# First steps of attention: another order for the first projections, the keys' transposes and the rotations, the first modulation unit ahead of them, and the weight ring to match

## The chip, the cores and the metric

The kernel runs on one core of a Trainium2 chip. The metric is the device time of one launch in microseconds (us). The core's engines are PE (TensorE, matrix products and transposes), DVE (VectorE), ACT (ScalarE), POOL (GpSimd) and SP (SyncE, which issues the transfers). Each engine works through its own list in order, and waits there for what an instruction needs from another engine or from a transfer.

## The reference, cut to what matters

One trunk layer for 128 context tokens and 512 latent tokens of width 1024:

```
u = rms_norm(h) * g_pre1 * (1 + scale1) + shift1
q, k, v, b, c, x, g_att, g_conv = split(u @ w_in)
q, k = rms_norm per head (q_norm, k_norm); axial rotary on latent tokens only
A  = softmax(q k^T / 8) v @ w_att_out     16 query heads, 4 key heads, head width 64
Bm = (b * dwconv3(c * x)) @ w_conv_out
h  = h + gate1 * rms_norm((sigmoid(g_att) * A + sigmoid(g_conv) * Bm) @ w_o)
h  = h + gate2 * rms_norm((silu(g) * val) @ w_down),   [g, val] = dwconv3(u2 @ w_up)
```

Latent tokens attend to all latent keys and 128 cached keys; context tokens read context tokens alone. The six modulation vectors (scale, shift and gate for both halves) come from `silu(c) @ w_ada + b_ada`, once for `c` and once for `c_ctx`. Outputs are both token groups and the context keys and values.

## The kernel before, in words

All tokens are five tiles of 128: tile 0 is context, tiles 1 to 4 are latent. Products are made in three passes on rounded operands (`mm3`, lines 159 to 162: high by high, low by high, high by low), so a weight unit is cut into a high part (a copy on ACT, `whi`) and a low part (a subtraction on DVE, `wlo`), out of a raw tile of 512 KB; there are three raw tiles and three of each part.

The prologue normalises the tokens, makes the first modulation and the keys and values of all tiles (`kv_mm`). Then comes the attention stage, whose lists on PE, ACT and DVE are written out by hand: they run in the order in which the code records them. Its parts:

- Per tile of keys: `k_rotate` (DVE, for some tiles the last sum on POOL) applies the rotary tables to the product in PSUM, `k_copies` (ACT) squares it and copies the values, `k_factors` (a reduction on DVE, then a scaling and a power on POOL, lines 460 to 462) gives the norm factor, `k_double` (line 561) writes the scaled keys twice side by side, on POOL for tiles 1 and 2 (line 564), on ACT for the others (line 567). `k_into` transposes them on PE (line 371), then `k_done` makes the high part on ACT (line 377: KCH, KH) and the low part on DVE (line 378: KCL, KL).
- Per tile of queries of one head group: `q_part` is the projection on PE (24 products of 256 columns for eight blocks of the width; lines 160 to 162), `q_rotate` the rotary on DVE with its sum on POOL (lines 447 to 450), `squares` on ACT (line 454) and `factors` as for keys, `q_turn` the transposes on PE (line 485) with high part on ACT (488) and low part on DVE (491). The first three query tiles of group 0 go through `q_first`, `q_rotate_first` and `q_factors`.
- A `Step` makes the scores of 128 queries for two heads on PE (line 499), then `most` (maxima, DVE, lines 636 and 638), `exps` (ACT, line 651), `shares` (reciprocal on DVE, line 660, product on POOL, line 661), `turned` (five transposes on PE, line 674, and a copy, line 679) and, after both halves of the queries, `values` (line 698). Step 0 of a group is its context step (lines 631, 645, 656, 657, 669). The code calls a step (g, i): group g from 0 to 3, i from 0 to 8. A step transposes the probabilities of the step before it. Between these, steps carry the projections of later query tiles, `cut_hi` of a weight unit (lines 599 and 602, at the places listed in `CUTS`) and one modulation unit (`ada_use`).
- A modulation unit is two raw tiles of `w_ada` multiplied by the conditioning vectors on PE (`ada_mm`, line 212) and kept on DVE (copied on first use, line 231, afterwards added, line 233). 16 such units are spread over the attention stage.

Raw tiles are filled by SP in the order of the list `ring`: entries ("u", n) are weight units, ("a", n) are modulation tiles. Three loads are issued when the stage starts; each later one is recorded when a raw tile has been used (`ring_used`): two after a modulation unit, one after a low part. An entry waits on SP for the raw tile that it overwrites, and all later entries wait behind it. PSUM holds three double banks (`ps2`: scores, transposes of keys and probabilities) and two single banks (`ps1`: projections, transposes of queries, values, modulation).

The order around the change: `q_first(0)`, the keys' rotations, `k_double(0)`, `q_first(1)`, `k_into(0)`, `q_first(2)`, `k_into(2)`, `q_turn(0, 0)`, `k_into(4)`, then the projection of query tile 3 in two halves with the context step's scores and `k_into(1)` between, `k_into(3)`, `q_turn(0, 1)`, and step (0, 1). There `q_turn(0, 2)` stands right behind the scores. The first modulation unit stands at the end of step (0, 2).

Of the kernel before, what the change touches and what calls it, by code (L numbers as in the profile page):

```python
# [18 lines left out]
KT = 8  # L19
# [5 lines left out]
NKV = 4  # L25
# [39 lines left out]
def trunk_layer(ctx, tc, x_prompt, x_sample, cache_k, cache_v, c, c_ctx, w_ada, b_ada, g_pre1, g_post1, g_pre2,  # L65
# [93 lines left out]
    def mm3(out, ah, al, bh, bl, start, stop):  # L159
        PE.matmul(out, ah, bh, start=start, stop=False)  # L160
        PE.matmul(out, ah, bl, start=False, stop=False)  # L161
        PE.matmul(out, al, bh, start=False, stop=stop)  # L162
# [271 lines left out]
    with tc.tile_pool(name="att", bufs=2) as at:  # L434
# [37 lines left out]
        def q_part(pz, g, t, ks):  # L472
            sl = slice(t * 128, (t + 1) * 128)
            for k in ks:
                mm3(pz, UH[:, k, sl], UL[:, k, sl], *state["cut"][KT + 2 * g + k // 4].at(k % 4), k == 0, k == KT - 1)
# [6 lines left out]
        def q_turn(g, t, p=None):  # L482
            p = ps1() if p is None else p
            for i in range(2):
                PE.transpose(p[:, i * 128:(i + 1) * 128], qfs[g, t][:, 2 * i:2 * i + 2].rearrange("p h d -> p (h d)"), ident)
            src = p[:, 0:256].rearrange("p (i c) -> p i c", i=2)
            qh, ql = (x[g][:, :, t * 128:(t + 1) * 128] for x in (QH, QL))
            S.activation(qh, src, AF.Copy)

            def low():  # L490
                V.tensor_tensor(out=ql, in0=src, in1=qh.bitcast(F32), op=ALU.subtract)
            return low
# [15 lines left out]
        def ada_raws(a, b):  # L508
            return [("a", i) for i in range(2 * a, 2 * b)]

        ring = [("u", 10), ("u", 11)] + ada_raws(0, 4) + [("u", 12)] + ada_raws(4, 5) + [("u", 13)] + ada_raws(5, 8) + [("u", 14)]
        ring += ada_raws(8, 9) + [("u", 15)] + ada_raws(9, 13) + [("u", 16)] + ada_raws(13, 15) + [("u", 17)] + ada_raws(15, 16) + [("u", 18)]
        at_ring = [0, 0]

        def ring_load(upto):
# [13 lines left out]
        def ada_use(i):  # L529
            p = ada2_mm(i)  # L530
            ring_used(2)
            return lambda: ada2_keep(i, p, acc)
# [26 lines left out]
            factors(sqs.pop(t), rks[t])  # L559

        def k_double(t):
            if t in (1, 2):
                for i in range(2):
                    G.tensor_tensor(out=kds[t][:, :, i, :], in0=kfs[t], in1=rks[t].unsqueeze(2).broadcast_to((128, NKV, HD)), op=ALU.mult)
                return
            for h in range(NKV):
                S.activation(kds[t][:, h], kfs[t][:, h:h + 1, :].broadcast_to((128, 2, HD)), AF.Copy, scale=rks[t][:, h:h + 1])
            if t == 0:
                nc.sync.dma_start(new_v.rearrange("t h d -> t (h d)"), VV[:, 5, :])
                nc.sync.dma_start(new_k, kds[t][:, :, 0, :])  # L570

        def k_into(t):
            p = ps2()[:, 0:512]
            k_turn(t, kds[t], p)
            k_done(t, p)

        def q_first(t):
            pzs[t] = ps1()[:, 0:256]
            q_part(pzs[t], 0, t, range(KT))

        def q_rotate_first(t):
            q_rotate(pzs[t], 0, t)
            sqs["q", t] = squares(pzs[t])

        def q_factors(t):
            factors(sqs.pop(("q", t)), rq[0][:, t, :])
# [136 lines left out]
        k_copies(1)  # L723
        q_first(1)
        k_rotate(3)
        k_double(2)
        k_factors(1)
        k_copies(3)
        k_factors(3)
        q_factors(0)  # L730
        k_into(0)
        k_double(4)
        k_double(1)
        q_first(2)
        k_into(2)
        low = q_turn(0, 0, ps2())
        low()
        k_into(4)
        k_double(3)
        q_rotate_first(1)  # L740
        q_factors(1)


        pz = ps1()[:, 0:256]
        q_part(pz, 0, 3, range(4))
        last = Step(0)
        last.most(0)
        k_into(1)
        q_part(pz, 0, 3, range(4, KT))
        k_into(3)  # L750
        low = q_turn(0, 1, ps2())
        low()
        last.exps(0)
        last.shares(0)
        q_rotate_first(2)
        q_factors(2)
        q_rotate(pz, 0, 3)
        sq = squares(pz)
        after1, after2 = [], [lambda: factors(sq, rq[0][:, 3, :])]
        n_ada, halves = 0, []  # L760
        q_begin(1)
        CUTS = {(0, 1): 10, (0, 2): 11, (0, 8): 12, (1, 2): 13, (1, 8): 14, (2, 2): 15, (3, 2): 16, (3, 6): 17}
        for g in range(NKV):
            if g and g + 1 < NKV:
                q_begin(g + 1)
            for i in range(0 if g else 1, 9):
                low1, low2, late_hi, end = [], [], [], []
                st = Step(g) if i == 0 else Step(g, ((i - 1) // 4, (i - 1) // 2 % 2, (i - 1) % 2))

                first = {0: (g, 2), 1: None if g else (0, 2), 5: (g, 4)}.get(i)  # L770
                then = {2: (g, 3), 5: (g + 1, 0), 7: (g + 1, 1)}.get(i)
                if then and then[0] == NKV:
                    then = None
                if first:
                    low1.append(q_turn(*first))
                if i == 2:
                    hi, lo = values(g)
                    hi()
                    low1.append(lo)
                for h in range(1 if st.ctx else 2):  # L780
                    st.most(h)
                    st.exps(h)
                for f in low1 + halves:
                    f()
                halves = []

                qt = None
                if g + 1 < NKV and i in (3, 5, 7):
                    qt = (g + 1, (i - 3) // 2)
                elif i == 0 or i == (2 if g else 1):  # L790
                    qt = (g, 3 if i == 0 else 4)
                blk = (i - 3) // 2 if g + 1 == NKV and i in (3, 5, 7) else None
                if i in (4, 6, 8) or (i == 1 and g):
                    hi, lo = values(*((g - 1, 3) if i == 1 else (g, (i - 4) // 2)))
                    late_hi.append(hi)
                    low2.append(lo)
                if qt:
                    pz = ps1()[:, 0:256]
                    q_part(pz, *qt, range(4))
                if blk is not None:  # L800
                    c0, c1 = 256 * blk, min(256 * blk + 256, NTOK)
                    pz = ps1()[:, 0:c1 - c0]
                    gate_part(pz, c0, c1, range(4))
                st.shares(0)
                for f in after1:
                    f()
                copy = last.turned(0)
                if last.ctx:
                    copy()
                else:  # L810
                    copy(i == 2 or (qt is None and blk is None))
                for f in late_hi:
                    f()

                if qt:
                    q_part(pz, *qt, range(4, KT))
                if blk is not None:
                    gate_part(pz, c0, c1, range(4, KT))
                if not st.ctx:
                    st.shares(1)  # L820
                if (g, i) in CUTS:
                    low = cut_hi(CUTS[g, i])
                    if i == 2 and 0 < g < NKV - 1:
                        low2.append(lambda low=low: low(0, 512))
                        halves = [lambda low=low: low(512, 1024)]
                    elif i <= 2:
                        halves = [low]
                    else:
                        end.append(low)
                if then:  # L830
                    low2.insert(0, q_turn(*then))
                for f in low2:
                    f()
                for f in after2:
                    f()
                if not last.ctx:
                    last.turned(1)()
                after1, after2 = [], []
                if i in (4, 6, 8) or i == (1 if g else 2):
                    ada_use(n_ada)()  # L840
                    n_ada += 1
                for f in end:
                    f()
                if qt:
                    def rotation(pz=pz, qt=qt):
                        q_rotate(pz, *qt)
                        sq = squares(pz)
                        after2.append(lambda: factors(sq, rq[qt[0]][:, qt[1], :]))
                    if i == 2:
                        after1.append(rotation)  # L850
                    else:
                        rotation()
                if blk is not None:
                    S.activation(gate0[:, c0:c1], pz, AF.Copy)
                last = st
# [997 lines left out]
```

## Time and profile before

| what | value |
| --- | --- |
| median of 3 runs | 1165.7 us (1160.63 to 1167.91) |
| profiled execution | 1164.31 us |
| its span, first to last instruction | 1162.5 us |
| PE busy | 1127.4 us, 97% of the span |
| DVE, ACT, POOL busy | 792.5, 569.0, 152.8 us |
| TensorE clock granted, mean | 0.987 |
| moved by DMA | 129.58 MB |

The page names the engine, the source line, and the tile written and read; a busy time is a sum over instructions and says nothing yet of what sets the end. Idle time on PE with its releaser in brackets ("[3.01 <-ACT sq L454]") tells for how long PE stood and which instruction let it go on. The granted clock is 1.00 at full speed and 0.50 at half speed.

### The profile page before, as it was taken

How to read it: one execution, taken by the hardware profiler on the slowest of the kernel's cores; microseconds unless marked ns; L12 is line 12 of the kernel's file. 1: busy time of each engine (PE TensorE's matmuls, PEld its weight loads, DVE VectorE, ACT ScalarE, POOL GpSimd, SP SyncE). 2: the span in 40 equal slices, each digit the busy share in tenths (PEclk: the TensorE clock that was granted, in tenths of full speed). 3: DMA queues.
4: the chain of work that ended last, by engine and by line, in shares of the span. 5: the costliest groups of instructions: out<-in, count | busy, mean ns of one | idle time of the engine just before them, and what ended most of it. 6: DMA issues, size and time to landing. Idle time of an engine off the chain costs nothing. (4 is left out here: it accounts for less than half of the span.)

```text
span 1162.5 us, 19634 instructions
## 1 busy us (share of the span) xinstructions
PE 1127.4 (97%) x7949; PEld 1032.6 (89%) x7949; DVE 792.5 (68%) x1270; ACT 569.0 (49%) x978; POOL 152.8 (13%) x199
## 2 busy tenths in 40 slices
PE   7986999999999999999999999999999999999997
PEld 5775888887899999999999988999999999998785
DVE  4465666655554788988745447888877788778634
ACT  4254666665433544554542246555454555545432
POOL 1044565654100000000000012000000000000001
PEclk8988999999999999999999999999999999999999
DMA  9912243333322323323232543333332333315732
GB/s 274 261 46 66 85 125 108 92 110 93 99 73 63 95 74 91 92 73 97 86 109 73 199 144 123 98 114 114 102 101 90 95 114 103 113 60 165 245 102 90
DMA packets 181400, 129.58 MB, mean 111 GB/s; under 512 B 6274, under 2 KB 163518, under 8 KB 181310
## 3 DMA queue, kind: packets, MB, share of 16 engines
q1 hardware_dynamic: 181198, 128.30, 36.0%
q8 instruction: 62, 1.02, 0.4%
q14 instruction: 28, 0.23, 0.1%
q10 hardware_dynamic: 112, 0.04, 0.0%
HBM read 116.87 MB, written 11.45 MB: 110 GB/s over the span
## 5 line engine op out<-in xcount | busy, mean ns | idle before, releaser
L919 PE MATMUL b<-ZB,whi 128*128 128x322 f32 x1024 | 229.5, 311 | 1.7 <-DVE C L930 1.7
L919 PEld LDWEIGHTS b<-ZB,whi 128*128 128x128 f32 x1024 | 173.5, 189 | 5.5 <-DVE C L930 3.8
L919 PE MATMUL b<-ZB,wlo 128*128 128x322 f32 x512 | 159.4, 311 | 0.0
L919 PE MATMUL b<-MT,whi 128*128 128x320 f32 x608 | 134.2, 308 | 0.0
L919 PEld LDWEIGHTS b<-MT,whi 128*128 128x128 f32 x608 | 101.5, 188 | 0.0
L919 PEld LDWEIGHTS b<-ZB,wlo 128*128 128x128 f32 x512 | 96.2, 188 | 0.0
L919 PE MATMUL b<-MT,wlo 128*128 128x320 f32 x304 | 93.8, 308 | 0.0
L661 POOL TENSOR_TENSOR pr<-pr,sm 128x640 f32<-128x640 f32 x64 | 79.7, 1255 | 75.2 <-DVE sm L660 75.1
L906 ACT ACTIVATE whi<-SUM 128x1024 fp32r<-128x1024 f32 x40 | 42.2, 1055 | 81.6 <-DVE SUM L1373 79.2
L1403 DVE SCALAR_TENSOR_TENSOR Y<-C,cffn,Y 128x642 f32<-128x642 f32 x88 | 77.6, 884 | 1.8 <-ACT Y L1398 0.2
L135 DVE TENSOR_TENSOR wlo<-raw,whi 128x1024 fp32r<-128x1024 f32 (+1 forms) x33 | 36.1, 1094 | 60.8 <-ACT whi L134 60.4
L651 ACT ACTIVATE pr<-s,mx,rq 128x640 f32<-128x640 f32 x64 | 56.7, 885 | 40.2 <-DVE mx L638 39.6
L160 PE MATMUL s<-whi,UH 128*128 128x256 f32 (+1 forms) x200 | 67.2, 336 | 6.0 <-ACT sq L454 3.5
L919 PE MATMUL b<-UH,whi 128*128 128x320 f32 x228 | 70.5, 309 | 0.0
L919 PE MATMUL b<-UL,whi 128*128 128x320 f32 x228 | 70.4, 309 | 0.0
L919 PE MATMUL b<-UH,wlo 128*128 128x320 f32 x228 | 70.2, 308 | 0.0
L636 DVE TENSOR_REDUCE mx<-s 128x1 f32<-128x640 f32 x64 | 52.5, 821 | 23.1 <-PE s L499 22.7
L910 DVE TENSOR_TENSOR wlo<-raw,whi 128x1024 fp32r<-128x1024 f32 (+1 forms) x51 | 50.4, 1019 | 25.2 <-ACT whi L906 24.4
L906 ACT ACTIVATE whi<-WB 128x1024 fp32r<-128x1024 f32 x38 | 40.1, 1056 | 54.8 <-DVE WB L1014 54.8
L927 ACT ACTIVATE p<-b 128x322 f32<-128x322 f32 (+1 forms) x78 | 34.3, 439 | 62.1 <-PE b L919 62.1
L161 PE MATMUL s<-wlo,UH 128*128 128x256 f32 (+1 forms) x200 | 63.2, 316 | 0.4 <-DVE wlo L602 0.4
L162 PE MATMUL s<-whi,UL 128*128 128x256 f32 (+1 forms) x200 | 60.8, 316 | 0.0
(309 smaller groups left out, 2942.6 us busy)
## 6 DMA issues: line engine op xcount, KB each, us to landing
raw<-in_w_in_dram SPq DMA_DIRECT2D x48, 512.0 KB, 3.7
RAW<-in_w_up_dram SPq DMA_DIRECT2D x40, 512.0 KB, 3.9
raw<-in_w_ada_dram SPq DMA_DIRECT2D x32, 512.0 KB, 4.0
raw<-in_w_down_dram SPq DMA_DIRECT2D x22, 512.0 KB, 4.3
araw<-in_w_ada_dram SPq DMA_DIRECT2D x16, 512.0 KB, 6.7
actd<-Y SPq DMA_DIRECT2D x18, 321.0 KB, 2.4
AFB<-actd SPq DMA_DIRECT2D x18, 321.0 KB, 5.4
raw<-in_w_conv_out_dram SPq DMA_DIRECT2D x9, 512.0 KB, 4.0
```

The costliest lines, as they stand in the source:

```text
L135: V.tensor_tensor(out=lo[:, :n], in0=raw, in1=hi[:, :n].bitcast(F32), op=ALU.subtract)
L160: PE.matmul(out, ah, bh, start=start, stop=False)
L161: PE.matmul(out, ah, bl, start=False, stop=False)
L162: PE.matmul(out, al, bh, start=False, stop=stop)
L636: V.tensor_reduce(out=mx, in_=self.sc[h], axis=AX.X, op=ALU.max, negate=True)
L651: S.activation(pr, self.sc[h], AF.Exp, bias=mx, scale=rs, accum_out=sm)
L661: G.tensor_tensor(out=pr, in0=pr, in1=sm.broadcast_to((128, NTOK)), op=ALU.mult)
L906: S.activation(to[0], raw, AF.Copy)
L910: V.tensor_tensor(out=lo, in0=raw, in1=hi.bitcast(F32), op=ALU.subtract)
L919: PE.matmul(out, p[:, ws], q[:, k, :], start=start and k == 0 and n == 0, stop=stop and k == 3 and n == 2, skip_group_check=True)
L927: S.activation(t, pair[j][b], AF.Copy)
L1403: V.scalar_tensor_tensor(out=y, in0=crows(j)[i][:, d:d + NACT], scalar=cffn[:, 44 * d + o:44 * d + o + 1], in1=y, op0=ALU.mult, op1=ALU.add)
```

## The change

- `k_double(2)` runs on ACT as four scaled copies and no longer on POOL; it is recorded after `k_factors(3)` and `q_factors(0)`.
- The first modulation unit (`ada_use(0)`) is recorded right behind it, ahead of `k_into(0)`, and no longer at the end of step (0, 2). `q_rotate_first(1)` follows `k_into(0)`; `q_factors(1)` follows `q_first(2)`.
- The second half of the projection of query tile 3 goes behind `k_into(3)` and `q_turn(0, 1)`; `q_rotate_first(2)` goes ahead of `shares`.
- In step (0, 1) the projection of query tile 4 is made in one piece, and `q_turn(0, 2)` follows it.
- The ring begins with the two tiles of the first modulation unit. Unit 16 comes two modulation tiles earlier, and is cut in step (2, 8) instead of (3, 2).
- Cuts in a step with i = 2 always have their low part made in two halves, one in the step and one in the next; the cut in (0, 1) has its low part at the end of the step instead of in the next one.

```diff
-        ring = [("u", 10), ("u", 11)] + ada_raws(0, 4) + [("u", 12)] + ada_raws(4, 5) + [("u", 13)] + ada_raws(5, 8) + [("u", 14)]
-        ring += ada_raws(8, 9) + [("u", 15)] + ada_raws(9, 13) + [("u", 16)] + ada_raws(13, 15) + [("u", 17)] + ada_raws(15, 16) + [("u", 18)]
+        ring = ada_raws(0, 1) + [("u", 10), ("u", 11)] + ada_raws(1, 4) + [("u", 12)] + ada_raws(4, 5) + [("u", 13)] + ada_raws(5, 8)
+        ring += [("u", 14)] + ada_raws(8, 9) + [("u", 15)] + ada_raws(9, 12) + [("u", 16)] + ada_raws(12, 15) + [("u", 17)]
+        ring += ada_raws(15, 16) + [("u", 18)]
...
         def k_double(t):
-            if t in (1, 2):
+            if t == 1:
...
         k_rotate(3)
-        k_double(2)
         k_factors(1)
         k_copies(3)
         k_factors(3)
         q_factors(0)
+        k_double(2)
+        ada_use(0)()
         k_into(0)
+        q_rotate_first(1)
         k_double(4)
         k_double(1)
         q_first(2)
+        q_factors(1)
         k_into(2)
         low = q_turn(0, 0, ps2())
         low()
         k_into(4)
         k_double(3)
-        q_rotate_first(1)
-        q_factors(1)
-
         pz = ps1()[:, 0:256]
         q_part(pz, 0, 3, range(4))
         last = Step(0)
         last.most(0)
         k_into(1)
-        q_part(pz, 0, 3, range(4, KT))
         k_into(3)
         low = q_turn(0, 1, ps2())
         low()
+        q_part(pz, 0, 3, range(4, KT))
         last.exps(0)
+        q_rotate_first(2)
         last.shares(0)
-        q_rotate_first(2)
         q_factors(2)
...
-        n_ada, halves = 0, []
+        n_ada, halves = 1, []
-        CUTS = {(0, 1): 10, (0, 2): 11, (0, 8): 12, (1, 2): 13, (1, 8): 14, (2, 2): 15, (3, 2): 16, (3, 6): 17}
+        CUTS = {(0, 1): 10, (0, 2): 11, (0, 8): 12, (1, 2): 13, (1, 8): 14, (2, 2): 15, (2, 8): 16, (3, 6): 17}
...
-                first = {0: (g, 2), 1: None if g else (0, 2), 5: (g, 4)}.get(i)
+                first = {0: (g, 2), 5: (g, 4)}.get(i)
...
+                start = g == 0 and i == 1
                 if qt:
                     pz = ps1()[:, 0:256]
-                    q_part(pz, *qt, range(4))
+                    q_part(pz, *qt, range(KT if start else 4))
+                if start:
+                    low2.append(q_turn(0, 2))
...
-                if qt:
+                if qt and not start:
                     q_part(pz, *qt, range(4, KT))
...
-                    if i == 2 and 0 < g < NKV - 1:
+                    if i == 2:
                         low2.append(lambda low=low: low(0, 512))
                         halves = [lambda low=low: low(512, 1024)]
-                    elif i <= 2:
-                        halves = [low]
                     else:
                         end.append(low)
...
-                if i in (4, 6, 8) or i == (1 if g else 2):
+                if i in (4, 6, 8) or (i == 1 and g):
                     ada_use(n_ada)()
                     n_ada += 1
```

## The prediction

> **What bounds the kernel now.** I read the page's slices first.
>
> ```profile
> span 1162.5 us, 19634 instructions
> ...
> PE   7986999999999999999999999999999999999997
> ...
> PEclk8988999999999999999999999999999999999999
> ```
>
> PE is busy nearly throughout. A slice is 29.1 us; the fourth (87 to 116 us) shows 6 for PE and 8 for its clock: the first steps of attention, where the change lies. So I asked PE's waits for two stretches, 60 to 116 us and 114 to 300 us (the rest of attention).
>
> ```profile
> PE s L212 <- DMA raw<-in_w_ada_dram: 4.0, 1, 4.0
> PE s L160 <- ACT sq L454: 3.5, 2, 3.0
> PE s L485 <- POOL qf L450: 1.9, 1, 1.9
> PE s L499 <- DVE KL L378: 1.3, 1, 1.3
> PE s L674 <- issue: 0.7, 1, 0.7
> PE s L161 <- DVE wlo L602: 0.4, 1, 0.4
> ```
> ```profile
> PE s L162 <- DVE wlo L602: 2.7, 1, 2.7
> ```
>
> In the first steps PE stands for 11.8 us, in the other 186 us for 2.7 us. Behind that, PE sets the pace, so time won or lost in the first steps passes on in full. Idle time has a second price, which the clock shows over stretches of 3.41 us:
>
> ```profile
> 81.00:84.41 3.41, 3.41 (x22) 3.07 (x22) 0.31 (x1) 0.00 (x0) 1.50 (x3) 0.50 0.02 5
> 84.41:87.83 3.42, 3.42 (x18) 3.42 (x17) 1.24 (x3) 0.60 (x1) 0.00 (x0) 0.50 0.00 0
> 87.83:91.24 3.41, 2.03 (x18) 1.47 (x16) 1.30 (x5) 2.63 (x10) 0.02 (x1) 1.00 0.00 0
> 91.24:94.65 3.41, 1.18 (x8) 0.94 (x9) 2.86 (x10) 1.23 (x4) 3.24 (x5) 1.00 0.00 0
> 94.65:98.07 3.42, 3.42 (x18) 3.42 (x18) 1.56 (x6) 2.62 (x6) 2.61 (x3) 0.50 0.00 0
> 101.48:104.89 3.41, 1.43 (x23) 0.90 (x21) 3.38 (x9) 3.39 (x7) 1.13 (x1) 1.00 0.02 7
> 104.89:108.31 3.42, 0.63 (x12) 0.60 (x16) 0.33 (x2) 0.14 (x1) 2.55 (x4) 0.50 1.00 292
> ```
>
> The columns after the length are PE, PEld, DVE, ACT and POOL busy, then the granted clock. The clock changes at the edges of these stretches only. Where PE was busy for 1.18 of 3.41 us (35%) or 1.43 (42%), the next stretch has half clock; after 2.03 (59%) it does not. The Trainium skill (TensorE: Matmul & The Clock Gate, Part 1) has the same free-running window of 3413 ns.
>
> **The change part by part.** Times are on the clock of the trace. Up to the first row here PE's list is the same in both kernels; the other rows are step (0, 1)'s and step (0, 4)'s scores, and one whole modulation unit.
>
> ```profile
> 71.84 0.64 PE L371 MATMUL s<-ident,room 128*128 128x128 f32 x4
> ...
> 80.26 0.39 PE L160 MATMUL s<-whi,UH 128*128 128x256 f32 x1 [3.01 <-ACT sq L454]
> ...
> 89.76 0.65 PE L499 MATMUL s<-KH,QH 64*128 64x320 f32 x2 [1.29 <-DVE KL L378]
> ...
> 115.89 0.42 PE L499 MATMUL s<-KH,QH 64*128 64x320 f32 x2
> ...
> 120.52 1.08 PE L212 MATMUL s<-raw,s 128*32 128x128 f32 x32
> ```
> ```profile
> 53.57 8.76 SPq L142 DMA_DIRECT2D raw<-in_w_in_dram  x2
> ...
> 103.69 0.37 SPq L206 DMA_DIRECT2D raw<-in_w_ada_dram  x1
> ```
> ```profile
> DMA to landing us min/median/max: 3.6/4.8/7.3
> ```
> ```profile
> 71.89 1.02 POOL L462 TENSOR_TENSOR rk<-ssq,mhalf 128x4 f32<-128x4 f32 x1
> ```
> ```profile
> 73.19 1.07 DVE L460 TENSOR_REDUCE ssq<-sq 128x4 f32<-128x256 f32 x3
> ```
> ```profile
> 73.45 0.60 ACT L377 ACTIVATE KCH<-s 128x512 fp32r<-128x512 f32 x1
> 75.59 1.28 ACT L567 ACTIVATE room<-room,rk 128x128 f32<-128x128 f32 x4 [1.54 <-POOL rk L462]
> ```
>
> *Modulation unit in front, ring.* The ring's first two loads leave SP by 62.3 us; now they carry the modulation tiles. Landing even 7.3 us later (last row: all modulation loads), they are there before 71.84, so the unit costs its 1.0 us of PE and no wait. In the old place its second tile could be issued only at 103.69, when unit 10 was cut: that is the wait of 4.0 us, and it goes. What queues now on SP behind the unit is unit 11's load (issued about 72.8, cut at 97: 24 us) and the next two modulation tiles (the last issued about 93.3, behind unit 10's low part; needed in step (0, 4), after 104). Both are hidden. The copy of the unit on DVE waits for PE (72.9) with KCL and the rotary queued behind it, but DVE is there only at 74.2.
>
> *q_first(2).* It took the PSUM bank of query tile 0; now it takes the bank of the modulation unit, freed by the copy at line 231 (0.29 us), which stands on DVE behind the three reductions that end at 74.26. PE: unit to 72.9, `k_into(0)` to 73.5, then 1.0 us idle, `q_first(2)` 74.5 to 77.5. The 3.0 us wait for the squares goes, since the squares are long done when the next projection asks for that bank.
>
> *k_double(2) on ACT.* Two POOL products of 0.6 us leave POOL, so later norm factors come 1.2 us earlier there; four ACT copies (1.28 us, as in the row) start when the factor is done (72.91) and ACT free (73.5). Queued behind them on ACT is KCH, now 74.7 to 75.3 instead of 73.45; behind it on DVE KCL, then the rotary of query tile 1 (76.0 to 76.7), behind that its squares, `k_double(4)` (to 78.3) and the high part of tile 2's keys. PE asks for `k_double(4)` only at 78.35, so this is covered by `q_first(2)`; without that cover it would cost 1.2 us.
>
> The rest goes by these durations (groups of 60 to 130 us):
>
> ```profile
> L651 ACT ACTIVATE pr<-s,mx,rq 128x640 f32<-128x640 f32 x11 | 9.7, 885 | 9.7 <-DVE mx L638 9.5
> ...
> L599 ACT ACTIVATE whi<-raw 128x1024 fp32r<-128x1024 f32 x2 | 2.1, 1049 | 0.0
> ```
> ```profile
> L636 DVE TENSOR_REDUCE mx<-s 128x1 f32<-128x640 f32 x12 | 9.8, 820 | 3.8 <-PE s L499 3.8
> ...
> L378 DVE TENSOR_TENSOR KL<-s,KH 128x512 fp32r<-128x512 f32 x5 | 3.4, 688 | 5.7 <-ACT KH L377 5.7
> ...
> L602 DVE TENSOR_TENSOR wlo<-raw,whi 128x1024 fp32r<-128x1024 f32 x2 | 2.4, 1218 | 0.0
> ```
>
> *Keys and step (0, 1).* Three transposes end at 78.95, half a projection at 80.5, the context scores at 81.25, `k_into(1)` and `k_into(3)` at 82.35. `q_turn(0, 1)` waits for the bank that tile 1's low part frees: high part 0.60 (as KCH) and low part 0.69, in turn behind each transpose, 83.25: 0.9 us idle. Turn and second half of tile 3's projection end at 85.2; they cover the key's and query's low parts (83.8, 84.5), so step (0, 1)'s scores start at 85.2, without the 1.3 us wait, against 89.76. The whole projection of query tile 4 (86.2 to 89.15) then covers the POOL sum that `q_turn(0, 2)` waited 1.9 us for.
>
> *Steps (0, 2) and (0, 3).* Here something else is late. `q_turn(0, 2)`'s high part stands on ACT behind both exponentials (to 90.2): step (0, 2)'s scores start at 90.6, 0.6 us idle. Unit 10's parts (ACT to 92.0, DVE to 93.3) now stand ahead of query tile 4's rotary, whose squares (94.45) free the bank for `q_turn(0, 3)`: 1.6 us idle. The next transposes wait for the first exponential of that step (96.0, 1.2 us idle), step (0, 3)'s scores for the second and a copy on DVE (97.15, 0.45 us). In step (0, 3) the second half of unit 11's low part stands behind both maxima (102.2): 1.0 us. Then step (0, 4)'s scores start at 103.5, against 115.89: 12.4 us.
>
> A second count: old idle 11.8 us, plus work at half clock from 81.0 to 87.8, 94.65 to 98.07 and 107.7 (the end of the transfer's wait) to 111.7 (the next edge), 14.3 us of which at most half is lost, 7.15; less the new idle, 6.75 us. That gives 12.2. I take 12.
>
> *Clock.* The stretches 91.24 to 94.65 and 94.65 to 98.07 would have PE 53% and 52% busy in the new order, between the 42% that brought half clock and the 59% that didn't. Bounds are none and three stretches; one costs up to 3.41 / 2 = 1.7 us, three 5.1. I take one, being just nearer the 59%.
>
> *Unit 16 from (3, 2) to (2, 8).* Maxima mark the steps; (1, 3) and (3, 3) hold the same PE work but for the wait:
>
> ```profile
> 161.35 0.82 DVE L636 TENSOR_REDUCE mx<-s 128x1 f32<-128x640 f32 x1 [0.18 <-PE s L499]
> ...
> 166.80 0.82 DVE L636 TENSOR_REDUCE mx<-s 128x1 f32<-128x640 f32 x1 [0.91 <-PE s L499]
> ```
> ```profile
> 260.94 0.82 DVE L636 TENSOR_REDUCE mx<-s 128x1 f32<-128x640 f32 x1 [0.78 <-PE s L499]
> ...
> 270.73 0.82 DVE L636 TENSOR_REDUCE mx<-s 128x1 f32<-128x640 f32 x1 [5.05 <-PE s L499]
> ```
> ```profile
> 132.96 0.52 SPq L142 DMA_DIRECT2D raw<-in_w_in_dram  x1
> ```
> ```profile
> 142.83 1.06 ACT L599 ACTIVATE whi<-raw 128x1024 fp32r<-128x1024 f32 x1
> ```
>
> 9.79 against 5.45 us: the wait of 2.7 us for the low part behind the maxima, and the half clock after it, cost 4.3 us, and both go. The cut in (2, 8) is what (0, 8) does now: load issued at 132.96, high part at 142.83, 9.9 us of cover, and no PE wait there. The halved low part in (0, 2) is already priced above; moved modulation loads keep a step or two of cover, as from group 0 to 1 now.
>
> Sum: 12 + 4.3 − 1.7 = 14.6 us. The profiled execution took 1164.31 us (span 1162.5 and 1.8 around it): 1149.7. The median of the runs, 1165.7, is 1.4 above it, inside their spread of 7.3.
>
> **The rivals.**
> - No stretch falls to half clock: 16.3 us, 1148.0. For it: no new gap is over 1.6 us. The Trainium skill (same page, Why this matters) asks only that no gap exceed about 3 us. By that rule this rival holds; the trace disagrees, as gaps of 2.7 us already brought half clock.
> - The first steps stay a chain through DVE and ACT: three half-clock stretches (5.1 us) and 2 us more of hand-offs (two more waits like that for the first exponential), 9.2 us, 1155.1. For it: the new idle from 90 to 102 us is all of this kind. Against: one such wait after another must fall late.
> - Unit 16's wait stays, because its load or its parts come late in (2, 8): 12 − 1.7 = 10.3, 1154.0. Against: (0, 8) and (1, 8).
> - Slower: the short new waits keep PE under the limit in stretch after stretch, and the clock doesn't come back. At 1.7 us a stretch it decides from 10 stretches on (34 us); over 1% slower takes 17, 1177. The trace has two in a row at most.
>
> **How the numbers follow.** Forecast 0.44, no half clock 0.20, chained first steps 0.20, unit 16 late 0.08, clock 0.03, and 0.05 for something unseen that leaves it within 1%. 1% is 11.6 us, about what a measurement can tell from no change. Faster: 0.44 + 0.20 = 0.64; within 1%: 0.20 + 0.08 + 0.05 = 0.33; slower: 0.03. Predicted 1149.7; the range reaches from 1148.0 less 4 us (half the runs' spread of 7.3) to 1155.1 plus 2: 1144 to 1157.
>
> **What would show it.** Right: no PE wait on a transfer before 130 us; `q_first(2)` waits about 1 us for line 231; step (0, 1)'s scores near 85, step (0, 4)'s near 103.5; no low-part wait in group 3. Wrong: the squares again ahead of a projection at 77, PE waiting on the key's high parts, half clock over several stretches from 91 on, or steps behind (0, 4) longer than before.

## The result, and the profile after

The changed kernel takes 1148.24 us, the median of four runs (1147.35 to 1150.42); the kernel before, in four runs, took 1165.27. The ratio is 0.9861, with a 95% interval of 0.9826 to 0.9896: faster by 1.4%, some 16 us by the ratio and 17 us between the medians. The forecast was 1149.7 us.

The page of the changed kernel, against the lines of before:

```profile
span 1148.6 us, 19637 instructions
...
PE   6998999999999999999999999999999999999997
...
PEclk7999999999999999999999999999999999999999
```

The fourth slice shows 8 for PE and 9 for the clock, where it showed 6 and 8. The first slice shows 7 for the clock where it showed 8: that is the code ahead of the change, and it took 2.69 us longer in this profiled execution (the row behind the second query projection starts at 74.53 us, against 71.84; I call this the end of that projection). Times of the two traces are compared here after taking off these 2.69 us.

The waits of PE from 60 to 116 us in the changed kernel (instruction, what ended the wait; us in total, times, longest):

```profile
PE s L485 <- ACT sq L454: 1.3, 1, 1.3
PE s L675 <- issue: 1.3, 1, 1.3
PE s L485 <- DVE KL L378: 1.1, 1, 1.1
PE s L160 <- DVE tabk L231: 0.9, 1, 0.9
PE s L499 <- ACT QH L488: 0.7, 1, 0.7
PE s L160 <- ACT UH L351: 0.4, 1, 0.4
```

The transfer's wait (4.0 us), the squares' wait ahead of a projection (3.0) and POOL's (1.9) are gone. So is the one for the keys' low part ahead of step (0, 1)'s scores (1.3). The first five rows stand in their place, 5.3 us: four new ones, and the one ahead of the transposes, 1.3 us where it was 0.7. The last row lies ahead of the change. From 116 to 300 us there is no row any more.

PE's timeline of the changed kernel (start, length, both in us; a bracket is the idle time ahead of the row): the modulation unit, the waits, and the scores of steps (0, 1) to (0, 4).

```profile
74.53 1.08 PE L212 MATMUL s<-raw,s 128*32 128x128 f32 x32
...
77.11 0.38 PE L160 MATMUL s<-whi,UH 128*128 128x256 f32 x1 [0.91 <-DVE tabk L231]
...
85.66 0.41 PE L485 MATMUL s<-ident,qf 128*128 128x128 f32 x2 [1.07 <-DVE KL L378]
...
87.43 0.41 PE L499 MATMUL s<-KH,QH 64*128 64x320 f32 x2
...
93.11 0.42 PE L499 MATMUL s<-KH,QH 64*128 64x320 f32 x2 [0.75 <-ACT QH L488]
...
97.01 0.44 PE L485 MATMUL s<-ident,qf 128*128 128x128 f32 x2 [1.30 <-ACT sq L454]
...
98.73 0.74 PE L675 MATMUL s<-ident,pr 128*128 128x128 f32 x5 [1.28 <-issue]
99.61 0.53 PE L499 MATMUL s<-KH,QH 64*128 64x320 f32 x2
...
106.45 0.42 PE L499 MATMUL s<-KH,QH 64*128 64x320 f32 x2
```

The stretch from the end of the second query projection to the scores of step (0, 4) is called the first steps below. It takes 106.45 − 74.53 = 31.92 us. Before it was 115.89 − 71.84 = 44.05: 12.13 us less.

Clock and busy times over the clock's own stretches (PE, PEld, DVE, ACT, POOL busy, then the granted clock):

```profile
93.47:96.89 3.42, 2.23 (x25) 1.54 (x21) 2.73 (x7) 1.34 (x4) 3.25 (x4) 1.00 0.01 3
96.89:100.30 3.41, 1.86 (x15) 1.42 (x17) 2.73 (x8) 2.99 (x7) 1.98 (x4) 1.00 0.52 153
100.30:103.71 3.41, 3.41 (x20) 3.08 (x17) 2.86 (x6) 1.37 (x4) 2.36 (x3) 0.50 0.03 10
103.71:107.13 3.42, 3.42 (x32) 3.25 (x33) 1.75 (x6) 2.78 (x6) 2.20 (x3) 1.00 0.25 65
```

One stretch has half clock. In the stretch ahead of it PE was busy for 1.86 of 3.41 us (55%). Before, five had it in the same steps (two from 81.0 us, one from 94.65, two from 104.89).

The first maxima of steps (3, 3) and (3, 4) on DVE:

```profile
251.62 0.82 DVE L637 TENSOR_REDUCE mx<-s 128x1 f32<-128x640 f32 x1 [0.78 <-PE s L499]
...
256.83 0.82 DVE L637 TENSOR_REDUCE mx<-s 128x1 f32<-128x640 f32 x1 [1.32 <-PE s L499]
```

5.21 us, where it was 9.79. Of these 4.58 us, 0.13 are lost in step (3, 1) and 0.04 in small differences, so the gain in group 3 is 4.41 us. The other steps behind (0, 4) agree between the two traces within 0.05 us, but for (2, 8) and (3, 0), where 0.85 us move from the one to the other. So the whole difference is accounted for: 12.13 + 4.41 − 2.69 = 13.85, and the spans differ by 1162.5 − 1148.6 = 13.9 us.

### The profile page after: what moved, and what is told of

Same layout as the page of the kernel before. It is cut to its first block, busy times and chain, and to the rows that moved or that the text cites. A ratio compares the mean times of both kernels' runs of the same rounds, so it can differ in the third digit from the quotient of the medians.

```text
span 1148.6 us, 19637 instructions
## 1 busy us (share of the span) xinstructions
PE 1122.7 (98%) x7949; PEld 1029.0 (90%) x7949; DVE 793.2 (69%) x1271; ACT 569.8 (50%) x982; POOL 154.2 (13%) x197
```

## The experiments

Ten kernels: three parts of the change alone, four in which something is taken back out of it, one suspected cost by itself, both of two edits together, and a version that goes further. "First steps" is the stretch named above, in the one trace that each kernel has.

| kernel | ratio to before (95%) | first steps, us | step (3, 3), us |
| --- | --- | --- | --- |
| before | | 44.05 | 9.79 |
| changed | 0.9861 (0.9826 to 0.9896) | 31.92 | 5.21 |
| before, unit in front alone | 0.9966 (0.9954 to 0.9977) | 38.47 | |
| before, one rotation earlier | 0.9955 (0.9938 to 0.9972) | 40.11 | |
| before, with filling products | 0.9983 (0.9970 to 0.9995) | 41.39 | |
| before, unit 16 earlier | 0.9962 (0.9947 to 0.9976) | 45.52 | 5.21 |
| changed, unit 16 at its old place | 0.9859 (0.9843 to 0.9876) | 32.87 | 5.71 |
| changed, modulation unit at its old place | 0.9869 (0.9854 to 0.9884) | 31.94 | |
| changed, `k_double(2)` on POOL | 0.9859 (0.9844 to 0.9873) | 32.28 | |
| changed, unit 10's low part later | 0.9843 (0.9829 to 0.9858) | 29.60 | |
| both of: unit old, low part later | 0.9881 (0.9864 to 0.9897) | 35.61 | |
| going further | 0.9821 (0.9807 to 0.9836) | 28.59 | |

The ratios of the changed kernel's variants mostly overlap; what tells those apart is the stretch in the trace. That has a spread of its own: no edit of the kernel with unit 16 earlier touches the first steps, yet they take 45.52 us there for 44.05, with seven stretches of half clock for five; with unit 16 back in the changed kernel they take 32.87 for 31.92, with two for one. So a difference of under 1.5 us counts here only where the waits and the clock behind it are named.

**The modulation unit in front, alone.**

```diff
-        ring = [("u", 10), ("u", 11)] + ada_raws(0, 4) + [("u", 12)]
+        ring = ada_raws(0, 1) + [("u", 10), ("u", 11)] + ada_raws(1, 4) + [("u", 12)]
...
         q_first(1)
...
+        ada_use(0)()
         k_into(0)
...
-        n_ada, halves = 0, []
+        n_ada, halves = 1, []
...
-                if i in (4, 6, 8) or i == (1 if g else 2):
+                if i in (4, 6, 8) or (i == 1 and g):
```

> The kernel before with the first modulation unit put ahead of the first transposes and its two tiles ahead in the ring; the order of projections, transposes and rotations is the old one. Theory (the waits of the first steps are one chain; the unit fills the first gap, so the half clock after it goes too, and each part alone already removes most): first steps 34 to 36 us instead of 44.05, time down by 8 to 10 us. Rival (the parts add up; the unit is worth its transfer's wait of 4.0 us and the half clock behind it, the rest belongs to the order): first steps about 38 us, time down by 6 us.

Measured: 38.47 us, what the rival gave; the theory's 34 to 36 fell. The medians are 4.0 us apart. The transfer's wait is gone, but the squares' wait is nearly as long as before. The modulation's copy is waited for as in the changed kernel (0.91), and two short waits (0.8 and 0.2 us) have come where the tile was waited for. PE's timeline of this kernel:

```profile
82.72 0.39 PE L160 MATMUL s<-whi,UH 128*128 128x256 f32 x1 [2.89 <-ACT sq L454]
```

The unit, 1 us of work, took 0.12 us off the squares' wait, not 1 us. The squares of query tile 1 end a chain that PE's own `k_into(4)` begins: high part of key tile 4 on ACT, its low part and then the rotary on DVE, then the squares on ACT. Shift PE, and the squares shift too. So work put ahead of this loop did not shorten the wait in it; the next kernel puts the rotation elsewhere in the order, and there the wait goes.

The half clock behind that gap is gone here, though the gap is nearly as long. An edge of the clock's stretches cuts the gap in two; the stretch on either side keeps full clock:

```profile
78.26:81.67 3.41, 1.58 (x15) 1.34 (x13) 1.82 (x5) 2.45 (x7) 3.41 (x5) 1.00 0.19 56
81.67:85.09 3.42, 2.37 (x24) 2.23 (x24) 0.94 (x3) 0.45 (x2) 1.96 (x4) 1.00 0.00 0
```

So part of what this kernel wins is luck with the edges.

**One rotation earlier, alone.**

```diff
         k_into(0)
+        q_rotate_first(1)
...
         q_first(2)
+        q_factors(1)
...
         k_double(3)
-        q_rotate_first(1)
-        q_factors(1)
```

> The kernel before with one edit alone: the first query rotation of head pair 1 is issued right behind the first k_into, and its factors behind the first projections of head pair 2, so TensorE has work in the place where it waited 3.0 us for the squares. Theory: the 3.0 us wait and the half clock that followed it at 81 to 88 us go, the other waits (1.3, 1.9 and 4.0 us) stay; the stretch from the end of the second query projection to the scores of step (0,4), 44.05 us before, comes to 38.5 to 40.5 us, and the kernel is 4 to 5.5 us faster (ratio 0.995 to 0.9965). Rival: another wait (GpSimd for key tile 1, or the copy of the keys) takes its place; the stretch stays at 42 us or more and the kernel is at most 2 us faster.

Measured: 115.33 − 75.22 = 40.11 us, inside what the theory gave; the wait of 3.0 us is gone, the clock stays at 1.00 until 90 us. The rival was half right: POOL's work for key tile 1 is now waited for. PE's timeline:

```profile
84.69 0.66 PE L371 MATMUL s<-ident,room 128*128 128x128 f32 x4 [1.47 <-POOL room L564]
```

In the changed kernel this wait is gone, only in small part because POOL has less to do. POOL lets PE go on 9.47 us after the start of the first steps here, and 9.42 us after it in the changed kernel with `k_double(2)` back on POOL (below). PE asks for it at 8.00 us here, and at 9.06 there: the modulation unit and the wait for its copy, 1.9 us, stand ahead.

**What the half clock costs.** In the gap of 3.0 us the kernel before gets 17 products into columns of the context step's PSUM tile that this step doesn't use; nothing is left out.

```diff
         k_double(3)
         q_rotate_first(1)
         q_factors(1)
+        pctx = ps2()
+        for _ in range(17):
+            PE.matmul(pctx[:, 256:512], UH[:, 0, 0:128], state["cut"][KT].at(0)[0], start=True, stop=True)
...
-        last = Step(0)
+        last = Step(0, p=pctx)
```

> The kernel before with 17 products of 256 columns more on PE, whose results nothing reads, written into unused columns of the context step's score tile, ahead of the projection of query tile 3: they stand in the gap of 3.0 us in which PE waits for the squares. Theory (idle time has a second price, the half clock of the next stretches, and it is paid in PE's pace): no half clock between 81 and 88 us, first steps 41 to 42 us instead of 44.05, though PE does 2 us more work. Rival (in those stretches the other engines set the pace and the half clock costs nothing): first steps 44 us within 0.5; where the added products hold up the projection, more.

Measured: 41.39 us, 2.66 us less, by work that computes nothing. A row of PE's timeline and one of the clock's stretches:

```profile
80.17 2.30 PE L746 MATMUL s<-whi,UH 128*128 128x256 f32 x17 [0.88 <-DVE KL L378]
```
```profile
81.00:84.41 3.41, 3.41 (x33) 3.23 (x33) 1.20 (x5) 1.19 (x4) 3.24 (x6) 1.00 0.00 0
```

In the kernel before, PE ran 22 products from 81.00 to 84.41 us of the trace, at clock 0.50; here it runs 33 in these 3.41 us at 1.00, some of them the added ones. The projection behind the gap starts as late as before, 8.43 us after the start of the first steps against 8.42; the scores of step (0, 1) come at 14.89 against 17.92. So by then the half clock had cost 3.0 us, of which 2.66 are left at the end of the first steps. The edges alone don't explain it, as they did with the unit in front: here a stretch runs from 79.0 to 82.4 us, so without the products nearly the whole gap would lie in one stretch, as it did before. The second price of that one gap is shown: 2.66 us, beside the 3.0 us of the gap itself.

**Unit 16.** Alone on the kernel before, and taken back out of the changed kernel (there the low part stays in halves):

```diff
-        ring += ada_raws(8, 9) + [("u", 15)] + ada_raws(9, 13) + [("u", 16)] + ada_raws(13, 15) + [("u", 17)]
+        ring += ada_raws(8, 9) + [("u", 15)] + ada_raws(9, 12) + [("u", 16)] + ada_raws(12, 15) + [("u", 17)]
...
-        CUTS = {(0, 1): 10, (0, 2): 11, (0, 8): 12, (1, 2): 13, (1, 8): 14, (2, 2): 15, (3, 2): 16, (3, 6): 17}
+        CUTS = {(0, 1): 10, (0, 2): 11, (0, 8): 12, (1, 2): 13, (1, 8): 14, (2, 2): 15, (2, 8): 16, (3, 6): 17}
```

> The kernel before with one part of the change alone: weight unit 16 two modulation tiles earlier in the ring and cut in step (2, 8) instead of (3, 2). Theory (the two places of the change are separate, and this one removes the low part's wait and the half clock after it): step (3, 3) takes 5.2 to 5.5 us instead of 9.79, the first steps (end of the second query projection to the scores of step (0, 4)) stay at 44.05 us, and the time falls by 4.3 us, ratio about 0.996. Rival (the wait moves to where the unit is now cut): PE waits 2 to 4 us in step (2, 8) or (3, 0), and the time doesn't change.

> The changed kernel with unit 16 back at its old place in the ring and cut in step (3, 2), where the new rule makes its low part in two halves. Theory (the wait came from the whole low part standing behind both maxima, and half of it made a step earlier is enough for the first half of the gate's product): step (3, 3) takes 5.2 to 5.9 us and the time is that of the changed kernel within 1 us. Rival (the place decides): step (3, 3) takes over 9 us again, 4.4 us more than the changed kernel.

Measured: 5.21 us for step (3, 3) with the earlier place, and no wait of PE in (2, 8) or (3, 0), so the rival fell; the first steps, expected to stay at 44.05 us, took 45.52, as said under the table. With the old place and halves the maxima of the steps stand 5.71 us apart:

```profile
250.41 0.82 DVE L637 TENSOR_REDUCE mx<-s 128x1 f32<-128x640 f32 x1
...
256.12 0.82 DVE L637 TENSOR_REDUCE mx<-s 128x1 f32<-128x640 f32 x1 [1.50 <-PE s L499]
```

The halving alone takes 4.1 of the 4.6 us out of this step; the earlier place adds 0.5. Two edits that each would do stand together in the change. (The first steps of the two kernels, 45.52 and 32.87 us, hold two more and one more stretch of half clock. No edit touches them; the clock's edges lie elsewhere against the work in these executions.)

**The modulation unit back at its old place.**

```diff
-        ring = ada_raws(0, 1) + [("u", 10), ("u", 11)] + ada_raws(1, 4) + [("u", 12)]
+        ring = [("u", 10), ("u", 11)] + ada_raws(0, 4) + [("u", 12)]
...
-        ada_use(0)()
...
-        n_ada, halves = 1, []
+        n_ada, halves = 0, []
...
-                if i in (4, 6, 8) or (i == 1 and g):
+                if i in (4, 6, 8) or i == (1 if g else 2):
```

> The changed kernel with the first modulation unit back at the end of step (0, 2) and its tiles back behind units 10 and 11 in the ring; the new order of projections, transposes and rotations, the new cuts and unit 16 stay. Theory (the second tile is issued after unit 10's low part at the end of step (0, 1), and now lands while PE waits for other things): PE waits at most 2 us for the tile, first steps 33 to 35.5 us instead of 31.9, 1 to 3.5 us more than the changed kernel. Rival (parts add up): the transfer's wait of 4 us and its half clock come back whole, first steps about 38 us, 6 us more than the changed kernel.

Measured: 31.94 us, below the 33 to 35.5 of the theory, as long as the changed kernel itself, with no wait for the tile. That the sums are equal is chance: without the unit ahead, PE waits 1.49 us for `k_double(4)` on ACT, and no stretch has half clock. What counts is the wait that is missing. Three of its rows, from the timelines of DVE, SP and PE:

```profile
93.77 1.22 DVE L603 TENSOR_TENSOR wlo<-raw,whi 128x1024 fp32r<-128x1024 f32 x1 [0.69 <-ACT whi L600]
```
```profile
95.02 16.96 SPq L206 DMA_DIRECT2D raw<-in_w_ada_dram  x6
```
```profile
98.63 1.08 PE L212 MATMUL s<-raw,s 128*32 128x128 f32 x32
```

Unit 10's low part ends at 95.0, SP issues the tile's load at 95.02, and PE runs the unit's 32 products in one piece from 98.63. The early low part frees the tile in time. The unit in front isn't alone in removing the 4.0 us in the changed kernel; either would.

**Unit 10's low part back behind the next step's maxima**, in the changed kernel:

```diff
                     if i == 2:
                         low2.append(lambda low=low: low(0, 512))
                         halves = [lambda low=low: low(512, 1024)]
+                    elif start:
+                        halves = [low]
```

> The changed kernel with unit 10's low part made behind the maxima of step (0, 2), as before the change, instead of at the end of step (0, 1). Theory (in the new order it is this low part, ahead of query tile 4's rotary and of the maxima on DVE, that makes PE wait 1.30 us for the squares and 1.28 us for the exponential): the wait for the squares goes, the one for the exponential shrinks below 1 us, first steps 30 to 31.3 us, time down by 0.5 to 2 us against the changed kernel. Rival (DVE has the same work before the copy that step (0, 3)'s scores need, so only the wait's name changes): first steps 31.9 us within 0.5.

Measured: 102.60 − 73.00 = 29.60 us, 2.3 less than the change and a little below what the theory gave. PE's waits from 60 to 116 us in this kernel:

```profile
PE s L485 <- DVE KL L378: 1.1, 1, 1.1
PE s L160 <- DVE tabk L231: 0.9, 1, 0.9
PE s L499 <- DVE PT L680: 0.8, 1, 0.8
PE s L675 <- POOL rq L462: 0.8, 1, 0.8
PE s L499 <- ACT QH L488: 0.8, 1, 0.8
PE s L160 <- ACT UH L351: 0.6, 1, 0.6
```

The wait for the squares (1.30) is gone, the one ahead of the transposes is 0.79 for 1.28, a new one of 0.84 waits for the copy of the transposed probabilities, and no stretch has half clock, whose products took 1.35 us more (worked out below). 1.30 + 0.49 − 0.84 + 1.35 = 2.30. The waits alone are 0.95 us; the 1.35 hang on where the clock's edges lie.

**Both taken back**: the unit at its old place and the low part later.

> The changed kernel with the first modulation unit back at the end of step (0, 2), its tiles back behind units 10 and 11 in the ring, and unit 10's low part back behind the maxima of step (0, 2). Against the run with only the first two of these (31.94 us, no wait for the tile). Theory (the tile's wait depends on when unit 10's low part frees its raw tile; the unit in front and the early low part are two ways to the same end, and one of them is needed): PE waits 1.5 to 4 us for the tile at the end of step (0, 2), first steps 33.5 to 37 us. Rival (neither is needed once the order is right): first steps 32 us within 0.7.

Measured: 35.61 us, and the tile's wait is back. The same three rows of this kernel:

```profile
96.33 1.22 DVE L603 TENSOR_TENSOR wlo<-raw,whi 128x1024 fp32r<-128x1024 f32 x1
```
```profile
97.64 9.85 SPq L206 DMA_DIRECT2D raw<-in_w_ada_dram  x4
```
```profile
101.45 1.08 PE L212 MATMUL s<-raw,s 128*32 128x128 f32 x16 [3.88 <-DMA raw<-in_w_ada_dram]
```

With this all four combinations are measured: the unit in front and the early low part are alternatives, one of them is needed, the change has both, and the early low part is the dear one.

**`k_double(2)` back on POOL**, in the changed kernel:

```diff
         def k_double(t):
-            if t == 1:
+            if t in (1, 2):
```

> The changed kernel with the doubling of key tile 2 back on POOL as two products. Theory (the four copies on ACT are covered, and so is the POOL work that they replace): first steps (end of the second query projection to the scores of step (0, 4)) 31.5 to 33 us as in the changed kernel and its variants (31.92, 32.87), time the same within 1 us. Rival (without the move POOL is late with key tile 1 or with query tile 1's sum): PE waits for POOL before the transposes of key tile 1 or of query tile 1, first steps 1.2 us longer or more.

Measured: 32.28 us, 0.36 more, which is already there at step (0, 1)'s scores; the rival's wait comes, but short. PE's waits have just this row in addition:

```profile
PE s L371 <- POOL room L565: 0.4, 1, 0.4
```

**Going further**: the low part later (the edit shown above), and the copies of the first steps in another order.

```diff
-        k_factors(1)
         k_copies(3)
+        ada_use(0)()
+        k_factors(1)
         k_factors(3)
         q_factors(0)
         k_double(2)
-        ada_use(0)()
         k_into(0)
-        q_rotate_first(1)
         k_double(4)
+        q_rotate_first(1)
...
         k_double(3)
+        q_rotate_first(2)
...
+        q_part(pz, 0, 3, range(4, 6))
         low = q_turn(0, 1, ps2())
         low()
-        q_part(pz, 0, 3, range(4, KT))
+        q_part(pz, 0, 3, range(6, KT))
         last.exps(0)
-        q_rotate_first(2)
```

> The changed kernel with unit 10's low part moved behind the next step's maxima, and with the first steps' copies reordered: the copy of the modulation unit ahead of the three reductions, key pair 2's doubling behind the query factors and key pair 4's ahead of the rotation of pair 1, the rotation of pair 2 behind key pair 3's doubling, and half of the products left for step (0,3) ahead of its turn. Theory: the waits of 0.9 us for the modulation's copy and 1.1 us for the keys mostly go; the stretch from the end of the second query projection to the scores of step (0,4), 29.60 us with the low part moved alone and 31.92 in the changed kernel, comes to 27.0 to 28.5 us, and the ratio to the kernel before to 0.982 to 0.984. Rival: the copies' own chain through VectorE and ScalarE in steps (0,2) and (0,3) sets the pace, and the waits only move: 29.6 us within 0.5, ratio 0.984 to 0.985.

Measured: 103.19 − 74.60 = 28.59 us, 1.0 less than with the low part alone, and 1146.64 us, the lowest median here. PE's waits:

```profile
PE s L499 <- ACT QH L488: 1.2, 1, 1.2
PE s L675 <- POOL rq L462: 0.8, 1, 0.8
PE s L499 <- DVE PT L680: 0.8, 1, 0.8
PE s L160 <- ACT UH L351: 0.6, 1, 0.6
PE s L485 <- DVE KL L378: 0.4, 1, 0.4
PE s L499 <- ACT pr L652: 0.2, 1, 0.2
```

The modulation copy's wait is gone, the keys' is 0.4 for 1.1; in exchange `q_turn(0, 2)`'s high part is waited for 0.4 us longer, and an exponential for 0.2. The theory held for these waits, with 28.59 us just above its 27.0 to 28.5; the rival's chain through ACT in step (0, 2) gave part of it back. By the traces this kernel beats both: neither it nor the one with the low part alone has half clock in the first steps, and against the changed one it has nearly the same start (74.60 and 74.53 us) and a span 3.2 us shorter (1145.4 and 1148.6), with 3.3 won in the first steps. The intervals of the three ratios overlap.

## Why the prediction was right, and where it was not

*The first steps.* The forecast was 12 us, less 1.7 for a stretch at half clock, 10.3; measured 12.13, with such a stretch in it. Its single points hold too. Scores of steps (0, 1) to (0, 4) were forecast at 85.2, 90.6, 97.15 and 103.5 us; measured, less 2.69: 84.74, 90.42, 96.92 and 103.76. The new waits stand where they were put: 1.0 forecast and 0.91 measured ahead of `q_first(2)`; 0.9 and 1.07 ahead of `q_turn(0, 1)`; 0.6 and 0.75; 1.6 and 1.30 for the squares; 1.2 and 1.28 for the exponential. Two more that it put down, 0.45 ahead of step (0, 3)'s scores and 1.0 for unit 11's low part, don't show. This came from writing down, for every engine, the order that the change gives it, with durations from the trace before, and carrying the start times forward.

*Unit 16.* Forecast 4.3, measured 4.41. The mechanism was right but not minimal: the halves that the change gives every cut at i = 2 would have won 4.1 without the move.

*The clock.* This is the step that was mis-sized. One stretch at half clock came, as forecast, behind the second of the two stretches named: they were forecast at 53% and 52% busy and measured 65% and 55%, with edges 0.5 us earlier against the work. That it was one is partly luck: the same order in the kernel with unit 16 back had two, and the measure behind the forecast, the busy share of one stretch, doesn't settle the clock. In the kernel with the unit in front alone 46% kept full clock and 56% lost it, and in the kernel before the stretch from 84.41 had half clock behind one in which PE was busy throughout. Nor did the one stretch cost 1.7 us. From the scores of step (0, 3) to those of step (0, 4) the changed kernel takes 106.45 − 99.61 = 6.84 us without a wait; the kernel with the unit at its old place, at full clock there, takes 6.02 with a wait of 0.53, so 5.49 of work. Half clock lengthened the products by 1.35 us. But the forecast had in the same place a wait of 1.0 us for unit 11's low part, and slower products use up that time. The price on the path is, as an estimate from these figures, between 6.84 − 6.02 = 0.82 and 1.35 − 1.0 = 0.35 us. The working counted both in full: a loss at half clock is a loss only as far as PE was not going to wait in that stretch.

*The transfer's wait.* "It goes" was right, but the cause named is only one of two. The prediction put it down to the modulation unit in front, which does remove it alone. The early low part of unit 10 would have freed the tile as well, as the unit at its old place showed, and the prediction did not ask when the new order frees that tile. The same low part is what the prediction had seen from the other side, as the work ahead of query tile 4's rotary that makes PE wait 1.6 us; it did not see that with the unit in front nothing needed it there.

*`k_double(2)`.* Costed at nothing behind `q_first(2)`; that held, but `q_first(2)` alone doesn't cover it: with the unit at its old place PE waits 1.49 us for `k_double(4)`. The unit and the wait for its copy are needed too. Leaving `k_double(2)` on POOL costs 0.36 us.

*The rivals.* No half clock at all: one stretch had it. The Trainium skill (TensorE: Matmul & The Clock Gate, Why this matters for your kernels) asks for no idle gap over some 3 us. Here two gaps of 1.30 and 1.28 us in one stretch were enough, so the measurement goes against the rule in that form. The chained first steps (three stretches and two more hand-offs): one stretch, and no hand-off beyond those forecast, each at most 0.2 us longer. Unit 16's wait: gone. The clock that doesn't come back: one stretch, then 1.00.

*The total.* The sum was 14.6 us from the profiled execution, and 16.5 us came out of the changed stretches (12.13 + 4.41), where the sum without the clock's term is 16.3. The profiled execution after has 2.69 us of longer prologue, with the clock at 0.50 from 20 to 30 us where it was 0.68 in the same code before, so it shows 1150.42; the median, 1148.24, is nearer to the sum of the terms. So that the total came out within 1.5 us is partly luck: the prologue, the same code in all these kernels, ends at 71.84 to 75.22 us in their traces, and the clock's term was too large. Why the prologue's clock differs between executions of the same code stays open.

## What to carry to other kernels

- When a hand-written order changes, write each engine's list in its new order and carry start times through it with durations from the trace; it found the five waits that came within 0.3 us here, and put down two that did not come. Then ask of each removed wait whether two parts of the change remove it: one of them may be a pure cost, as the early low part was (2.3 us, 1.35 of them through the clock).
- Don't add a loss at half clock to a wait that follows it in the same stretch; the slower work covers the wait (of 1.35 us of longer products 0.35 to 0.82 were left here).
- A wait whose releaser hangs on the waiting engine's own earlier output moves along when work is put ahead of it (3.01 us became 2.89); put the work, or the releaser's input, inside the loop.

## What was not expected of the hardware

- Neither the longest gap nor the busy share of one stretch of 3.41 us settles the clock. Two gaps of 1.30 and 1.28 us (55% busy) brought half clock. A gap of 2.89 us that an edge cut in two (46% busy, then 69%) did not; one of 3.01 us that lay almost whole in one stretch did, for two stretches. What rule fits all of these stays open.
- The gap of 3.0 us in the kernel before cost, through the clock, 2.66 us beside its own length: 17 products that nothing reads, put into it, made the kernel that much shorter in these steps.
